# The first mixer's transposed probabilities: all copies out of PSUM by ScalarE

## The chip, the cores and the metric

The kernel runs on one core of one Trainium2 chip. The metric is device time in microseconds of one execution: three runs of the kernel before took 2435.21, 2437.50 and 2441.94 us, a median of 2437.5. A fourth execution was profiled; all rows below are from it. The engines are TensorE (PE, with its weight loads as PEld), VectorE (DVE), ScalarE (ACT), GpSimd (POOL) and SyncE (SP, which issues the weights' DMAs).

## The reference

Two blocks follow each other on 512 tokens of width 1024. The first is a gated convolution with an mLSTM and a feed-forward network. The second block has two layers, each with a mixer, an attention over 256 memory rows, an output projection and a feed-forward network. The first layer's mixer is sparse attention with three branches, twelve heads of 64 in four groups:

```python
p_s = _masked_softmax(s_s, mask_s[:, :, None])
o_s = jnp.einsum('bgrqk,bgqkd->bqgrd', p_s.astype(vg.dtype), vg)
...
p_w = _masked_softmax(s_w, mask_w)
o_w = jnp.einsum('bgrqk,bkgd->bqgrd', p_w.astype(vwc.dtype), vwc)
...
return gc[:, :, 0] * o_c + gc[:, :, 1] * o_s + gc[:, :, 2] * o_w
```

The second layer's mixer is a recurrence over the tokens (RWKV-7, twelve heads): `state = state * w_t + sa * b_t + v_t * k_t`, read out with `r_t`. Everything is float32.

## The kernel before

Activations lie transposed in SBUF, 128 channels to a tile of 128x512. A float32 product with a weight is three products of split operands (high by high, high by low, low by high); these are the dense products, with `wh` and `wl` in their names. Weights come through SyncE's queue; ScalarE makes `wh`, VectorE `wl`.

Each mixer has a projection of dense products, side work (the mixer itself) and the output projection `_wo` (L1765) in three parts: the first needs the results 0 and 1 of the mixer and the memory attention, the second needs 2 and 3, the third 4 and 5. Side work is written as generators in a list (`_Side`, L407). After every few dense products the planner lets the generator run whose inputs are due first; where `_wo` lacks a result, it only steps side work.

What is due when is told by the planner's own clock (`_Clock`, L246), which adds a modelled duration for every instruction on its engine as it is written (ScalarE and VectorE have different ones) and notes who wrote and read what. That clock runs through the whole program. Its times decide the order in which instructions are written, and every engine then executes its own instructions in that order.

The clock also decides on idle products. Inside a mixer, `keep_warm` (L533) issues a 128x512 product of a tile of zeros into a bank that nobody reads, either until the time at which the next side work is due, or until a count that the planner keeps is reached:

```python
while self.zps is not None and (self.pe + 300 < until or not (until or self.clock.hot(HOTF))):
    self.nc.tensor.matmul(self.zps, self.zero[:, 0:128], self.zero, start=True, stop=True)
```

The first mixer (`_nsa`, L1699) makes six items of two heads. Each has, for two branches and four blocks of 128 queries, a unit `_nsa_unit` (L1614), 48 in all: products with the keys, a minimum and an exponential, a division by the sum with the gate, transposes of the probabilities into PSUM, copies to SBUF, products with the values. A unit of query block b covers n = 128(b+1) keys. For b of 0 and 1 both heads' probabilities share one bank; for b of 2 and 3 there are two banks and two copies. The line `if (i2 + b) % 2` (L1650) gives the copies in turn to VectorE (`vcopy`) and ScalarE (`acopy`).

The second mixer (`_rwkv`, L2178) makes six pairs of heads (`_rw_pair`, L1973). The steps of a pair that the prediction speaks of, in order: preparation; products for a 64x64 block matrix; the block inverse `_rw_inv` (L1933), which goes to DRAM (`ltd`), comes back, takes 30 small VectorE steps and a ScalarE copy, and goes through DRAM (`img`) once more; transposes of v; two levels of products that complete the inverse; products that apply it; products with `eye`; a recurrence of seven steps, each a product and a VectorE multiplication with `fs`; the read-out, its statistics (VectorE, GpSimd's power, ScalarE), transposes, a gate product, and a split into high and low parts (`hl_g`, L594) that `_wo` takes.

All instructions of the mixers are recorded through one helper, so all have the line L365 in the profile; they are told apart by tiles and shapes. In names, s is an SBUF tile, b a PSUM bank, wh and wl the split weights, fs the recurrence's factors, st, mv and gt the statistics. The idle product is `b<-s` with one s.

Of the kernel before, what the change touches and what calls it, by code (L numbers as in the profile page):

```python
# [1613 lines left out]
def _nsa_unit(B, i, br, b, st, P, mix):  # L1614

    nc = B.nc
    t = i // 3
    n = 128 * (b + 1)
    ks, vs = ("ks", t) if br == 0 else ("kw", t), ("vs", t) if br == 0 else ("vw", t)
    while not ("po" in P and ks in st and vs in st):  # L1620
        yield
    k, v = st[ks], st[vs]
    sm = B.mp.tile([128, 4], F32, tag="sm", name="sm", bufs=8)
    one = n <= 256
    held = [B.sl.get() for _ in range(1 if one else 2)]
    pr = [held[0][:, 0:n], held[0][:, n:2 * n] if one else held[1][:, 0:n]]
    for hf in range(2):
        ps = B.ps.get()
        q = P["q"][hf][:, 128 * b:128 * b + 128]
        B.mm(ps[:, :n], q, k[hf][:, 0:n], True, False)  # L1630
        B.mm(ps[:, :n], q, k[2 + hf][:, 0:n], False, True)
        nc.vector.tensor_tensor_reduce(pr[hf], ps[:, :n], P["strip"][hf][:, S - n:], 1.0, 3.0e38,
                                       op0=OP.add, op1=OP.min, accum_out=sm[:, 2 + hf:3 + hf])
        B.act(pr[hf], pr[hf], AF.Exp, bias=sm[:, 2 + hf:3 + hf], scale=-1.0, accum=sm[:, hf:hf + 1])
        B.ps.put(ps)
    yield
    g = 12 * (br + 1) + 2 * i
    nc.vector.reciprocal(sm[:, 0:2], sm[:, 0:2])
    B.tt(sm[:, 0:2], sm[:, 0:2], st["gts"][:, b, g:g + 2], OP.mult)
    for hf in range(2):  # L1640
        B.ts(pr[hf], pr[hf], sm[:, hf:hf + 1])
    yield
    ph = [B.sl.get() for _ in held]
    pt = [ph[0][:, 0:n], ph[0][:, n:2 * n] if one else ph[1][:, 0:n]]
    for i2 in range(len(held)):
        ps = B.ps.get()
        w = 2 * n if one else n
        for o in range(0, w, 128):
            B.tr(ps[:, o:o + 128], held[i2][:, o:o + 128], B.ident)
        if (i2 + b) % 2:  # L1650
            B.vcopy(ph[i2][:, :w], ps[:, :w])
        else:
            B.acopy(ph[i2][:, :w], ps[:, :w])
        B.ps.put(ps)
    B.sl.put(*held)
    yield
    P["n"][b] -= 1
    po = P["po"]
    for kb in range(b + 1):
        for hf in range(2):  # L1660
            B.mm(po[64 * hf:64 * hf + 64, 128 * b:128 * b + 128], v[:, kb, 64 * hf:64 * hf + 64],
                 pt[hf][:, 128 * kb:128 * kb + 128], False, sum(P["n"]) == 0 and kb == b)
    B.sl.put(*ph)
    if sum(P["n"]) == 0:
        B.sl.put(*P["q"], *P["strip"])
        yield
        mix[i] = yield from B.hl_g(po)
        B.ps.put(po)
# [30 lines left out]
def _nsa(B, xg, factors):  # L1699
# [9 lines left out]
    def project(n, ps):  # L1709
        t = B.sl.get()  # L1710
        if n == 18:
            B.tt(t[0:36], ps[0:36], rb[0:36], OP.mult)
            B.ps.put(ps)
            B.ts(t[0:36], t[0:36], B.col("gate_b", 0, 0, 36), None, OP.add)
            B.side.add(_nsa_gates(B, t, st))
        elif n in (19, 20) or n < 6:
            B.stt(t, ps, -0.125, rb, OP.mult, OP.mult)
            B.ps.put(ps)
            if n >= 19:
                B.side.add(_mem_att(B, 0, n - 19, t, cross), 6)  # L1720
            else:
                P = {"n": [2] * 4}
                B.side.add(_nsa_comp(B, n, t, st, P), 6)
                for br in range(2):
                    for b in range(3, -1, -1):
                        B.side.add(_nsa_unit(B, n, br, b, st, P, mix), 4 if b > 1 else 2)
        else:
            B.tt(t, ps, rb, OP.mult)
            B.ps.put(ps)
            nm, e = {6: "kc", 8: "vc", 10: "ks", 12: "vs", 14: "kw", 16: "vw"}[n - n % 2], n % 2  # L1730
            if nm in ("vs", "vw"):
                B.side.add(_tok_major(B, t, st, (nm, e)))
            elif nm in ("ks", "kw"):
                B.side.add(_stack_k(B, t, st, (nm, e)), 4)
            else:
                st[nm, e] = t
                if n == 9:
                    B.side.add(_compress(B, st), 4)
# [552 lines left out]
```

## Time and profile before

| what | value |
|---|---|
| median of three runs | 2437.5 us |
| profiled execution, its time | 2441.78 us |
| its span, first to last instruction | 2440.0 us |
| first mixer's units and projection in the span | about 1040 to 1262 us |
| second mixer, from its last projection to the third part | about 1770 to 2052 us |
| TensorE busy / granted clock, mean | 96% / 0.987 |
| VectorE, ScalarE, GpSimd busy | 59%, 38%, 13% |

A matmul's end is modelled and the next one begins before it, so a row's duration of about 0.4 us for a 128x512 product is not its share of TensorE's time; the distance between starts is. A float32 product that is not split stands as two instructions in the trace; a transpose stands as one.

### The profile page before, as it was taken

To read this page: it belongs to the slowest core of one execution; us is meant where nothing else is said; L and a number is where in the kernel's file an instruction comes from. 1 tells how busy PE (TensorE), PEld (TensorE's weight loads), DVE (VectorE), ACT (ScalarE), POOL (GpSimd) and SP (SyncE) were. 2 spreads that over 40 slices of the span, in tenths; PEclk is the share of its full clock that TensorE was granted. 3 is DMA by queue.
4 is the path that set the end of the run, shared out by engine and by line. 5 is a ranking of instruction groups with operands and counts; after the bars stand their busy time and mean duration, and the time that the engine had idled before them with its cause. 6 is when DMAs were issued, how large, how long until landed. Compare 5 with 4: busy or idle time off the path is not lost. (4 is left out here: it accounts for less than half of the span.)

```text
span 2440.0 us, 35941 instructions
## 1 busy us (share of the span) xinstructions
PE 2351.7 (96%) x14466; PEld 1919.4 (79%) x14466; DVE 1449.4 (59%) x2785; ACT 921.7 (38%) x1546; POOL 310.4 (13%) x291
## 2 busy tenths in 40 slices
PE   6999999899999999999999999999989899999997
PEld 5878887677888888877778888888868687888886
DVE  7977875776433335578885434446785666543443
ACT  5365455244222233346453222234343324322322
POOL 4333334200000002201001000021111200000000
PEclk9999999999999999999999999999998999999998
DMA  8222222744433323412213233244332141333322
GB/s 276 90 77 68 78 78 84 267 149 147 130 87 112 95 84 112 169 55 76 64 35 126 86 107 102 85 141 144 124 84 58 44 109 44 95 88 112 95 83 81
DMA packets 124711, 252.52 MB, mean 103 GB/s; under 512 B 48060, under 2 KB 54636, under 8 KB 124544
## 3 DMA queue, kind: packets, MB, share of 16 engines
q1 hardware_dynamic: 76096, 211.64, 27.9%
q0 software_dynamic: 10288, 32.48, 4.0%
q10 hardware_dynamic: 38160, 6.10, 1.4%
q8 instruction: 113, 1.85, 0.3%
q14 instruction: 54, 0.44, 0.1%
HBM read 234.43 MB, written 15.75 MB: 103 GB/s over the span
## 5 line engine op out<-in xcount | busy, mean ns | idle before, releaser
L365 PE MATMUL b<-s,wh 128*128 128x512 f32 (+1 forms) x5456 | 1687.5, 391 | 18.2 <-DVE s L365 11.4
L365 PEld LDWEIGHTS b<-s,wh 128*128 128x128 f32 x5456 | 1015.1, 189 | 234.4 <-DVE s L365 14.1
L365 PE MATMUL b<-s,wl 128*128 128x512 f32 (+1 forms) x2728 | 1060.1, 389 | 13.2 <-DVE wl L365 11.5
L365 PEld LDWEIGHTS b<-s,wl 128*128 128x128 f32 x2728 | 514.3, 189 | 122.0 <-DVE wl L365 15.1
L365 DVE TENSOR_TENSOR wl<-wr,wh 128x1024 fp32r<-128x1024 f32 (+2 forms) x313 | 356.2, 1140 | 221.1 <-ACT wh L365 219.8
L365 ACT ACTIVATE wh<-wr 128x1024 fp32r<-128x1024 f32 (+2 forms) x371 | 363.9, 983 | 231.2 <-PE b L365 176.9
L365 ACT ACTIVATE s<-s 128x512 f32<-128x512 f32 (+7 forms) x321 | 191.5, 611 | 626.1 <-DVE s L365 605.3
L365 DVE TENSOR_TENSOR s<-b,s 128x512 f32<-128x512 f32 (+3 forms) x314 | 196.9, 635 | 350.9 <-PE b L365 328.5
L365 DVE TENSOR_TENSOR s<-s,s 128x512 f32<-128x512 f32 (+12 forms) x466 | 239.3, 517 | 142.7 <-ACT s L365 132.7
L365 PE MATMUL b<-s,s 64*64 64x64 f32 (+5 forms) x4112 | 299.0, 257 | 16.5 <-DVE s L365 8.8
L365 PEld LDWEIGHTS b<-s,s 64*64 64x64 f32 (+2 forms) x4112 | 234.3, 145 | 78.4 <-issue 28.9
L365 ACT ACTIVATE s<-b 128x512 f32<-128x512 f32 (+4 forms) x227 | 107.1, 498 | 260.9 <-PE b L365 201.0
L365 DVE SCALAR_TENSOR_TENSOR b<-s,par,b 128x510 f32<-128x510 f32 (+28 forms) x288 | 193.2, 734 | 18.5 <-ACT b L365 17.2
L365 POOL TENSOR_TENSOR wl<-wr,wh 128x1024 fp32r<-128x1024 f32 x58 | 141.0, 2434 | 227.0 <-ACT wh L365 218.5
L365 POOL TENSOR_TENSOR s<-s,s 128x512 f32<-128x512 f32 (+1 forms) x38 | 44.3, 1187 | 428.9 <-ACT s L365 425.8
L365 PE MATMUL b<-ident,s 128*128 128x128 f32 (+1 forms) x520 | 76.7, 280 | 12.5 <-DVE s L365 8.4
L365 PEld LDWEIGHTS b<-ident,s 128*128 128x128 f32 (+1 forms) x520 | 59.5, 138 | 31.1 <-DVE s L365 13.1
L365 POOL TENSOR_TENSOR rs_t<-rs_t,mhalf 128x4 f32<-128x4 f32 (+1 forms) x8 | 10.7, 1334 | 560.7 <-DVE rs_t L365 560.7
L365 PE MATMUL b<-s 128*128 128x512 f32 x232 | 69.0, 426 | 0.0
L365 DVE SCALAR_TENSOR_TENSOR s<-s,par,s 128x512 fp32r<-128x512 f32 (+2 forms) x67 | 49.1, 747 | 30.5 <-ACT s L365 30.2
L365 ACT ACTIVATE s<-s,sm 128x512 f32<-128x512 f32 (+3 forms) x96 | 52.8, 552 | 36.8 <-DVE sm L365 36.3
L365 ACT ACTIVATE s<-b,par 128x512 f32<-128x512 f32 x54 | 37.3, 701 | 55.6 <-PE b L365 49.5
(161 smaller groups left out, 1138.5 us busy)
## 6 DMA issues: line engine op xcount, KB each, us to landing
wr<-in_w_in_dram SPq DMA_DIRECT2D x59, 512.0 KB, 3.5
s<-in_w_ada_dram SPq DMA_DIRECT2D x96, 256.0 KB, 5.4
wr<-in_fu_dram SPq DMA_DIRECT2D x44, 512.0 KB, 3.5
wr<-in_f0u_dram SPq DMA_DIRECT2D x44, 512.0 KB, 3.5
wr<-in_f1u_dram SPq DMA_DIRECT2D x44, 512.0 KB, 3.5
wr<-in_w_rw_dram SPq DMA_DIRECT2D x23, 512.0 KB, 3.9
wr<-in_w_nsa_dram SPq DMA_DIRECT2D x21, 512.0 KB, 3.6
wr<-in_w_o_dram SPq DMA_DIRECT2D x16, 512.0 KB, 3.6
```

The costliest lines, as they stand in the source:

```text
L365: r = f(*a, **k)
```

## The change

The choice of the engine is taken out; every copy is ScalarE's.

```diff
-        if (i2 + b) % 2:
-            B.vcopy(ph[i2][:, :w], ps[:, :w])
-        else:
-            B.acopy(ph[i2][:, :w], ps[:, :w])
+        B.acopy(ph[i2][:, :w], ps[:, :w])
```

36 copies move: all 24 that VectorE had of 128x512 and all 12 of 128x384. The planner's clock has other times from the first of them on, so what follows is written in another order, in both mixers. Without the idle products each engine but these two has as many instructions as before. Idle products: 232 before, 320 after. By place: first mixer 52 and 66; second mixer up to the first part's last products 131 and 166; in its last wait 49 and 88.

ScalarE's order, first units of the first mixer. The tiles s are the copies of transposed probabilities, b the banks they are in; `s,sm` rows are exponentials.

```order
 L365 ACTIVATE s_8047,sm<-s_8047,sm 128x128 x2
+L365 ACTIVATE s_8082<-b_8084 128x512
 L365 ACTIVATE s_8083<-b_8090 128x512
+L365 ACTIVATE s_8100<-b_8102 128x512
 L365 ACTIVATE s_8101<-b_8108 128x512
 L365 ACTIVATE s_8121<-b_8123 128x384
+L365 ACTIVATE s_8122<-b_8128 128x384
```

Both copies of a unit now stand one behind the other on ScalarE, and as many rows are gone from VectorE's order.

TensorE's order ahead of the first dense product of the second mixer's output projection, before. `b_12918<-s_12917` is the idle product, `k_11663` belongs to a pair's gate product, the 64x64 products to recurrences.

```order
L365 MATMUL b_16409<-k_11663,s_16192 128x512 x4
L365 MATMUL b_16418<-s_15232,s_15246 64x64
L365 MATMUL b_16418<-s_15232,s_14264 64x64
L365 MATMUL b_16457<-s_15728,s_15742 64x64
L365 MATMUL b_16457<-s_15728,s_14980 64x64
L365 MATMUL b_12918<-s_12917 128x512 x2
L365 MATMUL b_16463<-s_15231,s_15245 64x64
```

The same place after; the idle product is `b_12932<-s_12931`, the last row is the projection's first dense product.

```order
L365 MATMUL b_12932<-s_12931 128x512 x8
L365 MATMUL b_16254<-s_15500,s_16095 64x64 x16
L365 MATMUL b_16272<-k_11677,s_16088 128x512 x4
L365 MATMUL b_16281<-s_15269,s_15283 64x64
L365 MATMUL b_16281<-s_15269,s_14275 64x64
L365 MATMUL b_12932<-s_12931 128x512 x37
L365 MATMUL b_16324<-s_15992,s_15500 64x128 x8
L365 MATMUL b_16334<-s_15993,s_15500 64x128 x8
L365 MATMUL b_16367<-s_15850,wh 128x512
```

Runs of 8 and 37 idle products stand where there were 2.

TensorE's order at the end of the projection's second part, before: its last three dense products, and the fifth recurrence step of the last pair behind them.

```order
L365 MATMUL b_17702<-s_17198,wh 128x512
L365 MATMUL b_17702<-s_17199,wh 128x512
L365 MATMUL b_17702<-s_17198,wl 128x512
L365 MATMUL b_17710<-s_17210,s_17224 64x64
L365 MATMUL b_17710<-s_17210,s_16598 64x64
L365 MATMUL b_12918<-s_12917 128x512
```

The same place after: the second part's last dense products, and behind them the last pair's transposes of v.

```order
L365 MATMUL b_17410<-s_17231,wh 128x512
L365 MATMUL b_17410<-s_17230,wl 128x512
L365 MATMUL b_17427<-ident,s_15609 64x128 x4
L365 MATMUL b_17433<-ident,s_15609 64x128 x4
L365 MATMUL b_17441<-eye,s_15614 64x64 x2
```

Further on in the same wait, after: the last pair's second level, the fourth pair's gate product, and the products that apply the inverse, with idle products among them.

```order
L365 MATMUL b_12932<-s_12931 128x512 x6
L365 MATMUL b_17551<-s_17143,s_16839 64x64 x16
L365 MATMUL b_17569<-k_11677,s_17416 128x512 x4
L365 MATMUL b_17578<-s_17144,s_17485 64x64 x16
L365 MATMUL b_12932<-s_12931 128x512 x3
L365 MATMUL b_17600<-s_17439,s_17144 64x128 x8
L365 MATMUL b_17610<-s_17440,s_17144 64x128 x8
L365 MATMUL b_12932<-s_12931 128x512 x3
L365 MATMUL b_17623<-eye,s_15615 64x64
```

What stood ahead of the second part's last dense products, from the last pair's transposes to its fourth recurrence step, now stands behind them, and the last pair's block inverse comes 321 TensorE instructions (as the trace counts them, idle products left out) later than before.

## Rows read from the trace of the kernel before

**Rows 1.** The page's first part, busy time of each engine over the span.

```profile
PE 2351.7 (96%) x14466; PEld 1919.4 (79%) x14466; DVE 1449.4 (59%) x2785; ACT 921.7 (38%) x1546; POOL 310.4 (13%) x291
```

**Rows 2.** Busy time by stretches of the first mixer: stretch, its length, then PE, PEld, DVE, ACT, POOL busy with the number of instructions, granted clock, DMA share, GB/s.

```profile
1050.00:1100.00 50.00, 49.23 (x324) 38.06 (x323) 40.65 (x133) 26.61 (x71) 0.00 (x0) 1.00 0.12 37
1100.00:1150.00 50.00, 47.90 (x339) 36.07 (x338) 42.88 (x135) 33.05 (x96) 6.52 (x12) 1.00 0.25 82
1150.00:1200.00 50.00, 49.19 (x340) 37.38 (x339) 43.85 (x127) 27.61 (x69) 2.69 (x5) 1.00 0.21 64
1200.00:1250.00 50.00, 47.60 (x318) 36.70 (x317) 42.74 (x141) 25.09 (x70) 1.60 (x3) 1.00 0.11 35
```

**Rows 3.** Groups of instructions by form in the first mixer, 1040 to 1270 us: busy us, mean ns of one, idle time before them. The two copies of VectorE, the like of ScalarE, the idle products.

```profile
L365 DVE COPY s<-b 128x512 f32<-128x512 f32 x24 | 16.4, 683 | 0.8 <-PE b L365 0.8
...
L365 PE MATMUL b<-s 128*128 128x512 f32 x52 | 15.0, 407 | 0.0
...
L365 ACT ACTIVATE s<-b 128x512 f32<-128x512 f32 x22 | 12.6, 594 | 5.1 <-PE b L365 5.0
...
L365 DVE COPY s<-b 128x384 f32<-128x384 f32 x12 | 6.6, 550 | 1.5 <-PE b L365 1.5
...
L365 ACT ACTIVATE s<-b 128x384 f32<-128x384 f32 x12 | 5.9, 491 | 3.1 <-PE b L365 2.9
```

**Rows 4.** TensorE's waits in the same stretch: for whom, us in total, times, longest.

```profile
PE b L365 <- DVE s L365: 3.3, 5, 1.6
PE b L365 <- ACT s L365: 1.1, 3, 0.7
```

**Rows 5.** Idle products: the group over the whole run, and three stretches of the timeline (start, length, count), the first at full clock, the others behind the wait at 1826.

```profile
L365 PE MATMUL b<-s 128*128 128x512 f32 x232 | 69.0, 426 | 0.0
```

```profile
2040.21 6.19 PE L365 MATMUL b<-s 128*128 128x512 f32 x26
```

```profile
1827.61 2.91 PE L365 MATMUL b<-s 128*128 128x512 f32 x6
...
1830.85 0.79 PE L365 MATMUL b<-s 128*128 128x512 f32 x1
```

**Rows 6.** The second mixer: busy time and granted clock of four stretches (columns as in rows 2), and the two long waits of TensorE in the timeline, with the wait in brackets and who ended it.

```profile
1820.00:1830.00 10.00, 3.90 (x31) 2.86 (x22) 9.04 (x34) 2.76 (x7) 0.21 (x1) 0.80 0.01 2
1830.00:1840.00 10.00, 10.00 (x81) 7.22 (x80) 3.37 (x9) 2.54 (x7) 1.09 (x3) 0.51 0.31 80
...
1940.00:1950.00 10.00, 1.75 (x4) 1.46 (x5) 5.97 (x31) 2.96 (x9) 4.27 (x6) 0.61 0.13 27
1950.00:1960.00 10.00, 10.00 (x78) 7.44 (x78) 6.68 (x11) 2.48 (x4) 3.94 (x9) 0.88 0.97 286
```

```profile
1826.89 1.06 PE L365 MATMUL b<-ident,s 128*64 128x128 f32 x4 [6.10 <-DVE s L365]
```

```profile
1948.25 0.80 PE L365 MATMUL b<-s,wh 128*128 128x512 f32 x1 [10.63 <-DVE s L365]
```

**Rows 7.** VectorE's timeline ahead of that second wait's end: the small steps of an inverse, another pair's statistics, the wait for GpSimd, the low part.

```profile
1934.71 8.15 DVE L365 TENSOR_TENSOR s<-s,s 64x15 f32<-64x15 f32 x32
...
1943.55 1.15 DVE L365 BATCH_NORM_STATS2 st<-b 128x6 f32<-128x64 f32 x8
...
1947.43 0.17 DVE L365 SCALAR_TENSOR_TENSOR gt<-mv,gt 128x8 f32<-128x8 f32 x1 [1.85 <-POOL gt L365]
1947.51 0.68 DVE L365 TENSOR_TENSOR s<-s,s 128x512 fp32r<-128x512 f32 x1
```

**Rows 8.** Busy time and TensorE instructions of the stretch that begins with the last pair's inverse (columns as in rows 2).

```profile
1983.00:1998.00 15.00, 15.00 (x306) 12.18 (x306) 12.43 (x43) 3.60 (x8) 0.00 (x0) 1.00 0.33 82
```

**Rows 9.** The last pair's chain in the timelines of VectorE, ScalarE and TensorE: the inverse, its copy, out to DRAM, back, the first masked product; the fourth pair's transposes; the last pair's products after its second `eye` bank; the last step with `fs`, statistics, scaling; the third part's first dense product.

```profile
1983.17 7.54 DVE L365 TENSOR_TENSOR s<-s,s 128x512 f32<-128x512 f32 x31
...
2004.19 0.69 DVE L365 TENSOR_TENSOR s<-b,s 128x512 f32<-128x512 f32 x1 [0.79 <-PE b L365]
...
2036.84 0.29 DVE L365 TENSOR_TENSOR s<-b,fs 64x128 f32<-64x128 f32 x1 [0.54 <-PE b L365]
2040.32 1.15 DVE L365 BATCH_NORM_STATS2 st<-b 128x6 f32<-128x64 f32 x8 [3.19 <-PE b L365]
```

```profile
1990.75 0.88 ACT L365 ACTIVATE s<-s 64x256 f32<-64x256 f32 x2 [7.27 <-DVE s L365]
...
1991.59 0.58 ACTq L365 DMA_DIRECT2D img<-s  x1
...
1998.19 2.79 ACTq L365 DMA_DIRECT2D s<-img  x4
...
2044.48 2.47 ACT L365 ACTIVATE s<-b,gt 128x64 f32<-128x64 f32 x8 [10.54 <-DVE gt L365]
```

```profile
2022.17 0.28 PE L365 MATMUL b<-ident,s 128*128 128x128 f32 x1
...
2024.14 0.27 PE L365 MATMUL b<-eye,s 64*64 64x64 f32 x1
...
2052.02 0.61 PE L365 MATMUL b<-s,wh 128*128 128x512 f32 x2
```

## The prediction

> **What bounds the kernel now.** I read the busy line first [rows 1]: TensorE works 96% of the span, VectorE 59%, ScalarE 38%. Where TensorE is full, only what changes its own queue or leaves it waiting can change the time. So the second view is the stage that is edited, in stretches of 50 us [rows 2]: in the first mixer TensorE is busy for 47.6 to 49.2 of 50 us at a granted clock of 1.00, VectorE for 40.7 to 43.9, ScalarE for 25.1 to 33.1. VectorE is close to full and ScalarE is not. The third view, the list of waits, says what this costs: TensorE waited 3.3 us for VectorE and 1.1 us for ScalarE in the whole mixer [rows 4]. That is 4.4 us that a better share between the two could win there, and no more.
>
> The fourth view is the program's order, since the edit alone does not tell what moves. The idle products (keep_warm) are issued by the planner where its own clock sees TensorE wait, and that clock has other numbers once 36 copies change engine. In the order I count 232 idle products before and 320 after: 52 and 66 in the first mixer, 131 and 166 in the second mixer up to the second part of its output projection, 49 and 88 in the last wait there. All other TensorE work is the same in number. The second mixer is not edited at all and is planned anew all the same. So the fifth view is that stage: it holds the same kind of products, 232 of them in the whole run and never waited for [rows 5], it has waits in it, 6.10 us at 1826.89 and 10.63 us at 1948.25 [rows 6], and its end hangs on a chain and not on TensorE's load [rows 9].
>
> **The change part by part.** Removed from VectorE: 24 copies of 128x512 at 683 ns and 12 of 128x384 at 550 ns, 16.4 + 6.6 = 23.0 us [rows 3]. Added to ScalarE: the same at 594 and 491 ns, 14.3 + 5.9 = 20.1 us. Neither engine is the bound there, so both count only through waits. Half of VectorE's 3.3 us may go, with 23 us taken off the 170 that it works in those 200 us [rows 2]: -1.6. ScalarE now takes both copies of a long unit one behind the other, where the two engines worked side by side: 24 second copies, each late by up to 594 ns, are 14.2 us if every one of them were waited for; the next unit's products stand between a copy and its use, so I take 0.4. The 14 more idle products: 26 in a row take 6.19 us, so one costs (6.19 - 0.41) / 25 = 0.23 us at full clock, 0.41 being the mean duration of one [rows 3, 5]; 14 x 0.23 = 3.2 us in an engine that is full. Sum for the first mixer: 3.2 - 1.6 + 0.4 = +2.0. Bounds: -4.4 (all waits go, the idle products fall into gaps) and 3.2 + 14.2 = +17.4.
>
> On ScalarE and VectorE the Trainium skill speaks against this edit: "PSUM — Partial Sum Buffer", section "Specifications (TRN2)", says that the two can read PSUM in parallel at full rate, and its section on engine instructions that each queue is strictly first in, first out. By these the pair of copies would lose its overlap, which is the 14.2 us of the upper bound; the waits of 1.1 us for ScalarE [rows 4] speak for little of it.
>
> Second mixer, up to the second part of its projection: 35 more idle products, 35 x 0.23 = +8.1. But before the first product of the projection TensorE now has runs of 8 and 37 of them where there were 2, and in that place it stood still for 10.63 us [rows 6]. The rows of VectorE tell why: the 32 small steps of a pair's block inverse (8.15 us from 1934.71), the statistics of another pair, 1.85 us of waiting for GpSimd, and only then the low half that the projection waits for [rows 7]. The new order has the inverse earlier, and 45 x 0.23 = 10.4 us of idle products cover it. So the gap goes, and with it the slow clock behind it: the granted clock was 0.61 over 1.75 busy us and 0.88 over the next 10 [rows 6], 0.7 + 1.2 = 1.9 us lost. 8.1 - 10.6 - 1.9 = -4.4; I leave 1.4 us for what is late next and take -3. Bounds: +8.1 (the gap stays and all idle products are paid) and -10.5 (the 6.10 us gap goes too).
>
> The tail. The last of the six pairs falls behind. Before, the last products of the projection's second part stand among this pair's recurrence; now they stand ahead of its transposes, its two inverse levels and everything after. Its block inverse is reached 321 TensorE instructions later, counted in both orders; 306 took 15.0 us there [rows 8], so 15.7 us later. From that inverse to the third part's first product the chain lasted 2052.02 - 1983.17 = 68.9 us [rows 9]: inverse, copy, two DMA trips, levels, the recurrence, statistics, GpSimd, ScalarE, the last product. From the levels on, 48 dense products stood in it, 48 x 0.23 = 11.0 us, and the fourth pair's transposes with what followed them, 2022.17 to 2024.14, 2.0 us. In the new order these stand earlier, beside the inverse and its DMA trips, so the chain can shrink to 56. It doesn't shrink so far: 39 more idle products stand in it (9.0 us), and the fourth pair's statistics now queue behind the inverse on VectorE, with its transposes and then the last pair's behind them on TensorE (up to 4 us). Between 56 and 69 I take 63: 15.7 + 63 - 68.9 = +9.8. Bounds: +2.8 and +15.8.
>
> The sum is 2.0 - 3.0 + 9.8 = +8.8 us. Every duration is from the profiled execution: 2441.8 us, a span of 2440.0 and 1.8 around it, so it would become 2450.6. The median of the three runs is 4.3 us lower, and the prediction is made from that: 2437.5 + 8.8 = 2446. The order shows no DMA of SyncE moved past another; GpSimd's loads keep their sequence. That the edit does not do what it says is ruled out: VectorE keeps 1 of the 37 such copies, which belongs to another helper.
>
> **The rivals.** A: nothing comes of it. The work that is left for TensorE after the inverse is smaller by just the 321 instructions, so if the chain can run at 57 the tail costs 15.7 + 57 - 68.9 = +3.8; with -3 ahead of it and 0 in the first mixer, +0.8: 2438. For it: TensorE had no wait from 1983 to 1998 [rows 8], so work that is moved ahead is not lost. Against it: the inverse, its copy and its DMA trips alone are 21.0 us from 1983.17 to the first masked product at 2004.19 [rows 9].
>
> B: faster. The place is the gap before the projection and the mixer ahead: all 4.4 us of waits in the first mixer go, with its 14 idle products paid (3.2), the 10.6 us gap and the 1.9 us of slow clock go, the 35 idle products lie in gaps, and the last pair is not late: -4.4 + 3.2 - 10.6 - 1.9 = -13.7: 2424. It decides if the tail costs less than 6 us and the idle products are free. For it: VectorE is the fuller engine in the edited stage; the slow products, 0.42 us apart at 1827.61, follow a gap [rows 5]. The Trainium skill leans this way twice: "Perfetto Trace Analysis", section "Optimizing Scalar/DVE Operations", lets work go to ScalarE where VectorE is saturated, and "TensorE: Matmul & The Clock Gate", part 1, says that activity is what releases the throttle, by which more idle products buy clock. Against it: the clock was 1.00 in the edited stage [rows 2], and below it only in a few places of the later one.
>
> C: the idle products are paid in full, all 88 of them, 20.2 us, because TensorE had no gap where they now stand: 2458. For it: TensorE is 96% busy. Against it: 10.63 + 6.10 us of gaps lie in just this stage.
>
> **How the numbers follow.** What a measurement of this kernel can tell from no change is about 0.3%, 7.3 us: below 2430.2 is faster, above 2444.8 slower. The forecast has 0.46 (0.33 slower, 0.13 within), A 0.25 (0.22 within, 0.03 faster), B 0.13 (0.11 faster, 0.02 within), C 0.16 (slower). So slower 0.49, within 0.37, faster 0.14. The forecast's own range is 2438 to 2455. The whole range is 2429 to 2460: it takes in A, most of C and the near side of B, and leaves some 0.1 below and 0.05 above.
>
> **What would show it.** In the profile after: 24 and 12 more ScalarE copies out of PSUM and none such on VectorE in the first mixer, TensorE's waits there still 2 to 5 us; no wait near 10 us before the projection, with a run of 37 idle products in its place; the last pair's inverse on VectorE beginning after the second part's products have been issued or among the last of them; and the time between that part's last product and the third part's first growing by 15 us or more. Wrong would be: a gap before the projection as long as before (then C), the last part reached earlier than before (then B), or a first mixer that grows or shrinks by more than 5 us, which the waits don't allow.

## The result and the profile after

The changed kernel takes 2466.2 us (median of four runs, 2464.3 to 2467.9), the kernel before 2436.4 (four runs, 2430.9 to 2441.9): a ratio of 1.012, 95% interval 1.0106 to 1.0134, 29.8 us slower. The prediction said 2446 and a range up to 2460: the sign is right, the size is more than three times the forecast.

Where the time went can be followed at marks that both kernels have: the start of certain dense products in TensorE's timeline, found by counting in the order. A block is one tile of weights, 24 dense products; the output projection's first part has four of them, the second and the third have two each. Times in us from the span's start, in the profiled executions.

| mark | before | after | difference |
|---|---|---|---|
| first product of the first mixer's projection | 949.1 | 947.4 | -1.7 |
| first product of the first feed-forward network | 1271.5 | 1272.2 | +0.7 |
| last block of the second mixer's projection | 1769.1 | 1769.9 | +0.8 |
| output projection, first part, second block | 1962.6 | 1968.0 | +5.4 |
| output projection, second part, last block | 2021.5 | 2023.9 | +2.4 |
| output projection, third part | 2052.0 | 2075.7 | +23.7 |

The edited stage grows by 2.4 us and the unedited second mixer by 22.9 us; from there the difference stays within 1.2 us of that to the end. The two profiled spans differ by 22.5 us and the medians by 29.8, because the profiled execution of before was long in the second mixer (the last section).

The busy line of the changed kernel, which answers [rows 1]: TensorE's share is still 96%. Busy time alone tells nothing here, since idle products are counted in it.

```profile
PE 2374.4 (96%) x14554; PEld 1933.1 (79%) x14554; DVE 1430.6 (58%) x2749; ACT 938.9 (38%) x1582; POOL 310.1 (13%) x291
```

The edited stage of the changed kernel in stretches of 50 us (columns as in [rows 2]), then its waits of TensorE (as in [rows 4]) and three groups by form (as in [rows 3]):

```profile
1050.00:1100.00 50.00, 48.93 (x335) 37.92 (x335) 35.54 (x126) 31.81 (x86) 0.54 (x1) 1.00 0.10 33
1100.00:1150.00 50.00, 48.71 (x345) 37.57 (x345) 39.35 (x125) 35.21 (x101) 6.95 (x13) 1.00 0.26 83
1150.00:1200.00 50.00, 48.76 (x330) 37.63 (x327) 39.52 (x117) 29.38 (x72) 2.67 (x5) 1.00 0.18 63
1200.00:1250.00 50.00, 48.01 (x302) 35.26 (x300) 37.33 (x128) 28.22 (x78) 0.61 (x2) 1.00 0.11 35
```

```profile
PE b L365 <- ACT s L365: 2.0, 5, 0.6
PE b L365 <- DVE s L365: 1.8, 3, 0.9
PE b L365 <- DVE sm L365: 0.8, 1, 0.8
```

```profile
L365 PE MATMUL b<-s 128*128 128x512 f32 x66 | 18.4, 407 | 0.0
...
L365 ACT ACTIVATE s<-b 128x512 f32<-128x512 f32 x46 | 25.2, 593 | 1.4 <-PE b L365 1.2
...
L365 ACT ACTIVATE s<-b 128x384 f32<-128x384 f32 x24 | 10.4, 485 | 1.5 <-PE b L365 1.4
```

VectorE has lost its copies (170.1 busy us in these 200 became 151.7), ScalarE has 46 and 24 where it had 22 and 12, each as long as before. TensorE waits about as long as before (4.6 us against 4.4 in these rows), less for VectorE and more for ScalarE, and has 14 more idle products.

The second mixer ahead of the output projection, in TensorE's timeline of the changed kernel up to the projection's first product. Before, TensorE came to that product at 1936.41, and the 10.63 us wait of [rows 6] stood behind the projection's first four products; first before, then after:

```profile
1936.41 0.74 PE L365 MATMUL b<-s,wh 128*128 128x512 f32 x2
1936.99 0.40 PE L365 MATMUL b<-s,wl 128*128 128x512 f32 x1
1937.23 0.40 PE L365 MATMUL b<-s,wh 128*128 128x512 f32 x1
```

```profile
1907.56 0.66 PE L365 MATMUL b<-ident,s 128*128 128x128 f32 x4 [1.48 <-ACT s L365]
...
1910.85 0.33 PE L365 MATMUL b<-s,s 64*64 64x64 f32 x4 [1.55 <-ACT s L365]
...
1916.04 2.37 PE L365 MATMUL b<-s,s 64*64 64x64 f32 x32 [2.77 <-DMA s<-img]
...
1932.74 8.65 PE L365 MATMUL b<-s 128*128 128x512 f32 x37
1941.33 1.96 PE L365 MATMUL b<-s,s 64*64 64x128 f32 x32
1943.22 0.74 PE L365 MATMUL b<-s,wh 128*128 128x512 f32 x2
```

The long wait is gone, and 37 idle products take 8.65 us, ahead of the projection's first product and not behind it. Ahead of them are new waits, and TensorE is busy for 23.40 us of the 30 from 1900, at a granted clock of 0.83:

```profile
1900.00:1930.00 30.00, 23.40 (x465) 19.12 (x465) 13.27 (x42) 8.26 (x21) 7.65 (x13) 0.83 0.45 113
```

The last pair's chain in the changed kernel, to be read beside [rows 9]: VectorE's timeline, then ScalarE's, then TensorE's.

```profile
2009.32 6.94 DVE L365 TENSOR_TENSOR s<-s,s 64x15 f32<-64x15 f32 x30
...
2016.90 0.68 DVE L365 TENSOR_TENSOR s<-s,s 128x512 fp32r<-128x512 f32 x1
2017.50 1.15 DVE L365 BATCH_NORM_STATS2 st<-b 128x6 f32<-128x64 f32 x8
...
2021.25 0.17 DVE L365 SCALAR_TENSOR_TENSOR gt<-mv,gt 128x8 f32<-128x8 f32 x1 [1.86 <-POOL gt L365]
...
2035.19 0.69 DVE L365 TENSOR_TENSOR s<-b,s 128x512 f32<-128x512 f32 x1 [1.20 <-PE b L365]
...
2064.02 1.15 DVE L365 BATCH_NORM_STATS2 st<-b 128x6 f32<-128x64 f32 x8 [1.58 <-PE b L365]
```

```profile
2016.35 0.64 ACT L365 ACTIVATE s<-s 64x256 f32<-64x256 f32 x1 [6.72 <-DVE s L365]
2021.51 0.70 ACT L365 ACTIVATE s<-b,gt 128x64 f32<-128x64 f32 x2 [4.52 <-DVE gt L365]
2021.88 0.58 ACTq L365 DMA_DIRECT2D img<-s  x1
```

```profile
2017.63 0.50 PE L365 MATMUL b<-s,wh 128*128 128x512 f32 x1 [3.49 <-DVE s L365]
...
2075.69 0.62 PE L365 MATMUL b<-s,wh 128*128 128x512 f32 x2
```

The inverse begins at 2009.32, 26.1 us later than the group at 1983.17 of [rows 9]; from there to the third part it is 66.4 us where it was 68.9. (That group has another operation in front. Its 30 small steps begin at 1983.78, so on equal terms it is 25.5 us, and 66.4 where it was 68.2.)

```profile
1983.78 6.94 DVE L365 TENSOR_TENSOR s<-s,s 64x15 f32<-64x15 f32 x30
```

So the chain is nearly as long as before and starts late, when little other work is left beside it: the stretch from the last block of the second part to the third part is 51.8 us where it was 30.5. TensorE's row at 2017.63 shows the inverse also holding up the projection itself for 3.49 us, since the low half that it needs (VectorE's row at 2016.90) stands behind the 30 small steps.

### The profile page after: what moved, and what is told of

Same layout as the page of the kernel before. It is cut to its first block, busy times and chain, and to the rows that moved or that the text cites. A ratio compares the mean times of both kernels' runs of the same rounds, so it can differ in the third digit from the quotient of the medians.

```text
span 2462.5 us, 36157 instructions
## 1 busy us (share of the span) xinstructions
PE 2374.4 (96%) x14554; PEld 1933.1 (79%) x14554; DVE 1430.6 (58%) x2749; ACT 938.9 (38%) x1582; POOL 310.1 (13%) x291
## 5 line engine op out<-in xcount | busy, mean ns | idle before, releaser
L365 PE MATMUL b<-s,wl 128*128 128x512 f32 (+1 forms) x2728 | 1060.1, 389 | 12.8 <-DVE wl L365 11.2
L365 DVE TENSOR_TENSOR s<-b,s 128x512 f32<-128x512 f32 (+2 forms) x314 | 196.7, 636 | 367.2 <-PE b L365 345.2
L365 ACT ACTIVATE s<-b 128x256 f32<-128x256 f32 (+4 forms) x263 | 124.2, 508 | 238.8 <-PE b L365 191.6
L365 PE MATMUL b<-s 128*128 128x512 f32 x320 | 92.2, 418 | 0.0
L365 PE MATMUL b<-ident,s 128*128 128x128 f32 (+1 forms) x520 | 76.2, 279 | 15.9 <-DVE s L365 10.8
L365 PEld LDWEIGHTS b<-s 128*128 128x128 f32 x320 | 58.8, 192 | 14.0 <-issue 1.7
L365 DVE SCALAR_TENSOR_TENSOR s<-s,par,s 128x512 fp32r<-128x512 f32 (+2 forms) x67 | 49.1, 748 | 30.3 <-ACT s L365 30.0
```

The costliest lines, as they stand in the source:

```text
L365: r = f(*a, **k)
```

## The experiments

Three theories stood against each other. Order: the second mixer's new order costs the time, and the moved copies cost nothing. Engines: the copies on ScalarE, or the first mixer's 14 more idle products, cost it. Idle: the idle products are paid in full. Eight kernels were run, each beside the kernel before on the same chip (its median was 2434.7 in the first four, 2435.2 in the others).

**1. The edit, with the second mixer in the old order.** At the start of the second mixer the planner's clocks of the two kernels differ by the same 1535.3 ns on every engine that computes. `shift` adds it to all times that the clock holds, and its second argument brings the count of the planner's current stretch to that of before.

```diff
     B.ratio, B.lat = RRATIO, RLAT
+    B.clock.shift(1535.3, 3584.0)
```

> The edited first mixer as it stands (its engines and its order), but the planner's clock is moved on by 1535.3 ns where the second mixer begins, to what it reads there in the kernel before; by that the second mixer gets the order of before, instruction for instruction. Order theory (the new order of the unedited second mixer costs the time): the edit keeps only the 2.4 us by which the first mixer grew between the two traces, so 2438 to 2441 us, and TensorE reaches the third part of the projection about 30 us after the sixth block of the second part, as before. Engine theory (the copies on ScalarE cost, or 14 more idle products in the first mixer): near the changed kernel, 2460 to 2468.

Measured: 2435.2 us, ratio 1.0008 (0.9993 to 1.0022), 3 us below the expected 2438 to 2441; the third part comes 30.5 us after the projection's sixth block, which is the second part's last. The loss is gone although every copy runs on ScalarE and the first mixer has its new order. The engine theory falls.

**2. The kernel before, with the second mixer in the new order.**

```diff
     B.ratio, B.lat = RRATIO, RLAT
+    B.clock.shift(-1535.3, -3584.0)
```

> The kernel before with not one copy moved; only the planner's clock is set back by 1535.3 ns where the second mixer begins, to what it reads there in the changed kernel, so that the second mixer gets the changed kernel's order. Order theory: slower by the 23 to 27 us that lie in the second mixer, 2460 to 2464. Engine theory: no change, 2434 to 2440.

Measured: 2465.0 us, ratio 1.0121 (1.0105 to 1.0137), 30.3 us slower without a single copy moved. That is the whole loss. It is even somewhat more than the 23 to 27 us expected, which were read against a profiled execution that was itself long in this stage (the last section).

**3. The copies moved, the whole order as before.**

```diff
+        if (i2 + b) % 2:
+            B.acopy_as_v(ph[i2][:, :w], ps[:, :w])
+        else:
+            B.acopy(ph[i2][:, :w], ps[:, :w])
...
+    def acopy_as_v(self, out, in_):
+        self.tc.nc.scalar.activation(out, in_, AF.Copy, bias=0.0, scale=1.0)
+        self.clock.note("vector", "tensor_copy", (out, in_), {})
```

> All 36 copies run on ScalarE, but the planner is told that the second ones ran on VectorE, so that the order of the whole program and its 232 idle products are those of before. Order theory: within 3 us of before, 2434 to 2440; the sign says whether the moved copies by themselves help (VectorE waited for less) or hurt (the pair in series). Engine theory: near the changed kernel, 2455 or more.

Measured: 2429.7 us, ratio 0.9974 (0.9965 to 0.9984), 5.0 us faster: below the expected band. TensorE's waits in the first mixer of this kernel:

```profile
PE b L365 <- ACT s L365: 1.3, 3, 0.9
...
PE b L365 <- DVE s L365: 0.2, 1, 0.2
```

Beside [rows 4], the 3.3 us of waiting for VectorE are gone and ScalarE's 1.1 have become 1.3. So the edit does help in its own stage, and two ScalarE copies in series are almost never waited for. The traces show it in the stage itself, from the first product of its projection to that of the feed-forward network. It is 322.4 us in the kernel before and in runs 2 and 7 (old copies, old order), 317.7 in runs 3 and 8 (copies moved, old order) and 324.7 to 324.8 in the changed kernel and in runs 1, 4, 5 and 6 (copies moved, new order). So the moved copies are worth -4.8 us there, and the first mixer's new order costs 7.1 us; between the medians of runs 1 and 3 it is 5.4.

**4. Half of the second mixer's idle products left out.**

```diff
+            self.idle += 1
+            z = (self.zps, self.zero[:, 0:128], self.zero)
+            if self.thin and self.idle % 2:
+                self.clock.note("tensor", "matmul", z, {})
+            else:
+                self.nc.tensor.matmul(*z, start=True, stop=True)
```

> The changed kernel in its own order, but every second idle product of the second mixer is not issued (the planner still counts it): 127 of 254 are left, fewer than the 180 of before. Nothing reads an idle product, so no part of the result is left out. Idle theory (each idle product is paid in full at 0.23 us): 127 x 0.23 = 29 us less, 2437. Order theory (they stand in waits for the last pair's chain): 2460 to 2466, or a few us more if the granted clock falls in the waits.

Measured: 2457.7 us, ratio to the kernel before 1.0088 (1.0073 to 1.0103), 8.5 us less than the changed kernel. 8.5 / 127 = 0.067 us for each product left out, where one in a full engine would cost 0.23. Neither theory is met exactly. TensorE's waits from 1770 to 2080 us, and its busy time and granted clock there, say where the rest went; first the changed kernel, then this one:

```profile
PE b L365 <- DVE s L365: 13.9, 8, 5.6
PE b L365 <- ACT s L365: 7.7, 6, 2.2
```

```profile
1770.00:2080.00 310.00, 282.98 (x4553) 223.72 (x4554) 186.23 (x550) 98.56 (x229) 38.55 (x54) 0.96 0.25 62
```

```profile
PE b L365 <- DVE s L365: 22.7, 14, 5.6
PE b L365 <- ACT s L365: 12.8, 12, 3.4
```

```profile
1770.00:2080.00 310.00, 268.71 (x4462) 212.08 (x4461) 193.26 (x560) 102.70 (x235) 38.63 (x54) 0.93 0.26 65
```

Waits for VectorE and ScalarE grow by 8.8 and 5.1 us: about half of what was taken out comes back as plain waiting. The granted clock falls too, from 0.96 to 0.93; over the whole execution it is 0.984 to 0.985 in the four executions of this run and 0.987 to 0.988 in the four of the changed kernel. By these rows that costs 0.07 x 268.7 - 0.04 x 283.0 = 7.5 us, an estimate. Of 29.2 us taken out, 13.9 and 7.5 so come back, which leaves about the 8.5 that were won. So 0.067 us is a net price in this stage: most idle products stand in waits, and they also kept the clock up. At this price the 74 more of the second mixer are 5.0 us of the 30, an estimate.

**5. Only the last pair's priority raised.**

```diff
-                B.side.add(_rw_pair(B, p, [st.pop(i, None) for i in range(3)], R, mix), 0, 10 - p)
+                B.side.add(_rw_pair(B, p, [st.pop(i, None) for i in range(3)], R, mix), 0, 10 - p + 2 * (p == 5))
```

> The changed kernel with one number more: the sixth pair's priority in the second mixer is raised by 2, so that it goes ahead of the fifth where both are ready. Late-pair theory (of the 30 us, some 21 are the last pair's chain, which stands alone between the second and the third part of the projection, 51.8 us in the changed kernel against 30.5): that stretch falls below 30 us and the total to 2438 to 2455 us, although nothing is put back to the order of before. Rival (what was lost is a good order as a whole, and no single pair): 2460 or more.

Measured: 2441.4 us, ratio 1.0021 (1.0008 to 1.0035): one number recovers 24.9 of the 29.8 us, with 31 more idle products in the second mixer than the kernel before has (211 in place of 180). The inverse on VectorE, and TensorE's way to the third part, in this kernel:

```profile
1969.44 7.28 DVE L365 TENSOR_TENSOR s<-s,s 128x256 fp32r<-128x256 f32 x31
```

```profile
2042.13 6.31 PE L365 MATMUL b<-s 128*128 128x512 f32 x27
2048.28 2.04 PE L365 MATMUL b<-k,s 128*128 128x512 f32 x8
2050.16 1.75 PE L365 MATMUL b<-s 128*128 128x512 f32 x7
2051.75 0.62 PE L365 MATMUL b<-s,wh 128*128 128x512 f32 x2
```

The inverse begins some 40 us earlier than in the changed kernel (the group's 31 steps are one split and the 30 of the inverse), and the last stretch is 15.9 us in place of 51.8. What is left of it is one pair's statistics and gate, covered by 27 and 7 idle products. The first part's second block comes 196.8 us after the projection's last block, nearly as late as in the changed kernel (198.2; 184.7 in run 1), so what this run wins back it wins behind that mark.

**6. The last two pairs raised.** As in run 5, with `10 - p + 3 * (p > 3)`.

> The changed kernel with the priorities of the fifth and the sixth pair raised by 3, ahead of the third and fourth. Late-pair theory: the second part's dense products, which the first four pairs feed, now stand behind the last two pairs' work and fill what was the tail; the stretch between the second part's last product and the third part's first falls near 10 us, and the total below the kernel before, 2415 to 2435. Rival (no single pair; or the wait only moves ahead of the projection): 2445 or more.

Measured: 2431.5 us, ratio 0.9983 (0.9971 to 0.9995). The third part now follows the last block of the second after 5.4 us, its own length: nothing is waited for at the end any more. The projection starts later (198.8 us after the mark at the projection's last block, where the changed kernel needs 173.4), and the mixer ends earlier all the same.

**7. The kernel before at a third phase of the clock.**

```diff
     B.ratio, B.lat = RRATIO, RLAT
+    B.clock.shift(600.0, 0.0)
```

> The kernel before, not one copy moved; the planner's clock is moved on by 600 ns where the second mixer begins, a value that neither kernel has. Phase theory (where the planner's clock stands against its own fixed 3413 ns windows at that point decides the order, and the kernel before stands at a good place): slower, with another order and another loss, 2445 to 2465, and the last pair late again. Rival (the changed kernel's phase is a single bad one): 2432 to 2440.

Measured: 2467.4 us, ratio 1.0124 (1.0102 to 1.0147), a little above the expected band. A shift by a value that neither kernel has costs 32 us. So the changed kernel's phase is not a single bad one. The last stretch is 41.1 us here, and the second part ends 20 us late too.

**8. The good halves together:** run 3's copies, run 6's priorities, the clock of the changed kernel in the second mixer.

```diff
+            B.acopy_as_v(ph[i2][:, :w], ps[:, :w])
...
+    B.clock.shift(-1535.3, -3584.0)
...
+                B.side.add(_rw_pair(B, p, [st.pop(i, None) for i in range(3)], R, mix), 0, 10 - p + 3 * (p > 3))
```

> What the runs so far say is good, together: the 36 copies on ScalarE with the first mixer in the order of before (2429.7), and in the second mixer the clock and the priorities of the run with the last two pairs raised. Late-pair theory: that run's time less some 5 us, 2410 to 2430, below both kernels. If the two gains are one and the same (both only free VectorE): no better than the run with the last two pairs raised.

Measured: 2421.5 us, ratio 0.9936 (0.9917 to 0.9955), 13.7 us below the kernel before and 44.8 below the changed one. Its busy line shows TensorE at 97% of a span of 2419.7 us:

```profile
PE 2347.4 (97%) x14504; PEld 1924.2 (80%) x14504; DVE 1428.6 (59%) x2749; ACT 936.4 (39%) x1582; POOL 309.6 (13%) x291
```

The gain over run 6 is 10 us, twice the expected 5. Between the two traces it is 13.1 us: 7.0 in the first mixer, since run 6 has the changed kernel's order there (the expectation counted only the copies' 5), and 5.4 in the second mixer, whose order is the same in both; why that stage was shorter was not tried.

The second mixer of all ten kernels, from the projection's last block (which is 0), in us:

| kernel | first part | second part, last block | third part | last stretch | idle products in the last stretch | median |
|---|---|---|---|---|---|---|
| before | 167.4 | 252.4 | 283.0 | 30.5 | 49 | 2436 |
| after | 173.4 | 254.1 | 305.8 | 51.8 | 88 | 2466 |
| run 1 | 158.7 | 245.0 | 275.5 | 30.5 | 49 | 2435 |
| run 2 | 172.8 | 253.5 | 305.3 | 51.7 | 88 | 2465 |
| run 3 | 160.5 | 247.2 | 277.7 | 30.5 | 49 | 2430 |
| run 4 | 167.2 | 248.8 | 297.3 | 48.5 | 44 | 2458 |
| run 5 | 171.4 | 265.9 | 281.8 | 15.9 | 34 | 2441 |
| run 6 | 198.8 | 269.0 | 274.5 | 5.4 | 0 | 2432 |
| run 7 | 173.0 | 272.2 | 313.3 | 41.1 | 73 | 2467 |
| run 8 | 197.9 | 263.7 | 269.1 | 5.4 | 0 | 2421 |

Runs 5 and 6 plan the whole stage anew with their priorities, so they don't show that the last pair's lateness alone, with all else unchanged, is worth 25 us. They show that orders in which the last pair is early have no long last stretch and are fast, even with more idle products and a later projection.

## Why the prediction was right in sign and wrong in size

Most of the signs that the prediction named came out: the copies, TensorE's waits in the first mixer, the 37 idle products, the growth of the last stretch. They test the mechanism and not the sizes. Two steps failed, the front of the second mixer by its mechanism and the tail by its size. Against the profiled execution of before they missed by 7.6 and 8.5 us. Most of the rest lies in that profile itself: its second mixer was 5.2 and 7.5 us longer than the same order took in runs 3 and 1.

**First mixer, +2.0.** The traces give +2.4, but that is luck: two terms were both too small and cancel. The VectorE waits were priced at -1.6, and 4.4 was called all that could be won; run 3 shows 4.8 us in the stage (5.0 between the medians; by its interval, 1.6 to 3.5 per mille, 3.9 to 8.5 us). TensorE's waits for the two engines fell by only 2.9 of that, from 4.4 to 1.5; where the rest comes from is open. The 24 second copies in series were taken as +0.4 with an upper bound of 14.2 (13.0, since 12 of them are of 128x384 and take 491 ns); run 3 shows next to nothing (1.3 us of waits for ScalarE in place of 1.1). The rule that the prediction quoted from the Trainium skill ("PSUM — Partial Sum Buffer", section "Specifications (TRN2)") on the two engines reading PSUM side by side does not decide here: the overlap that it describes was given up, and run 3 is faster. Against that stands the new order of the first mixer, 7.1 us, where the prediction counted 3.2 for the 14 idle products and nothing for waits that the order brings: TensorE waits for 4.6 us in the changed kernel and for 1.5 in run 3.

**Front of the second mixer, -3.** This is the step that failed first: "So the gap goes, and with it the slow clock behind it." The gap went, and the 37 idle products are where they were said to be. But a gap that is filled by idle products is not time won, and they do not even stand in that gap's place: it stood behind the projection's first four products, they stand ahead of the first. That first product came 6.0 us later than in the profiled execution before (14.7 and 12.8 later than in runs 1 and 3). From there to the first part's second block the changed kernel takes 24.8 us where it was 26.2, because other side work filled what had been the gap. What mattered was when the next result arrived, and TensorE's useful work was late: the first part's second block came 4.6 us later than in the profiled execution before, not 3 earlier. Against runs 1 and 3, which have the old order at a higher granted clock there, it is 13.5 and 10.9 us. The new waits at 1907 to 1916 and the stretch at clock 0.83 stand in this part; no run took them out alone, and run 4 takes 5.2 us of the loss back by leaving out 83 idle products up to there. No view of before could show these waits. The honest bound for an unedited stage that is planned anew was far above +8.1.

**The tail, +9.8.** The mechanism was right: the last pair late, and the third part waiting for its chain. One sign was not met: the inverse was to begin among the last products of the second part or behind them, and it begins 3.7 us ahead of that part's first product, at 2013.06. The size was off in two terms. The term that was mis-sized most is "its block inverse is reached 321 TensorE instructions later", 15.7 us by the mean of [rows 8]. The inverse came 26.1 us later: 5.4 us of it was late already at the first part's second block, the other 20.7 make 0.064 us for an instruction, not 0.049. The price came from a stretch full of short 64x64 products (85% of its products; 68% and 72% in the two stretches below). The stretch just ahead of it in the same trace gives 0.061, and the changed kernel's way from the second block to the inverse 0.060, with TensorE busy throughout; first before, then after:

```profile
1962.60:1983.10 20.50, 20.39 (x335) 16.58 (x333) 12.86 (x38) 9.12 (x21) 2.78 (x3) 1.00 0.32 79
```

```profile
1968.00:2009.30 41.30, 41.30 (x685) 31.39 (x682) 27.14 (x67) 10.25 (x24) 4.48 (x7) 1.00 0.25 70
```

The second term is the chain, taken as 63 us between 56 and 69, which measured 66.4. In it, the queueing that was priced at up to 4 us is the 4.9 us between the end of the inverse's copy (2016.99) and its first DMA out (2021.88): ScalarE issues both, and another pair's scaling stands between, waiting for VectorE, which waits for GpSimd. (In [rows 9] the DMA follows the copies at once.) The pair whose transposes the prediction calls the fourth is the last but one; it counts from 0. From the first part's second block to the third part the loss is 18.3 us, above the term's bound of 15.8.

**The rivals.** C (all idle products paid in full) gave 2458 and was the nearest in size, for the wrong reason: run 4 shows 0.067 us net for one in the second mixer, at which 88 of them are 5.9 us and not 20.2 (an estimate). B was right on VectorE's waits, and in that idle products keep the clock up (run 4: 0.96, and 0.93 with half of them left out); its gain in the second mixer did not come. A's "the chain can run at 57" did not hold. What was missing was a rival of another kind: that the order before is a good one, so that a replanning of the second mixer can lose some tens of us by itself. Runs 2 and 7 show two such orders, at +30 and +32; how many orders are as good was not tried. For this a sign stood in the kernel itself: a clock with fixed steps that runs through the whole program, so that a shift by 1.5 us upstream reaches a stage that nobody edits.

## What to carry to other kernels

Where a planner's clock runs through the program, split an edit into what it does on the engines and what it does to the order, by telling the planner the old cost: here the first is worth -5 us and the second +35. A stage that is replanned without being edited deserves a wide range that leans to the slow side, and terms such as "this gap goes" should be priced by when the next needed result arrives and not by how TensorE fills the time. When the end of a stage hangs on the last of several equal chains, raise that chain's priority first: it was worth more here than all copies.

## What the runs showed of the hardware

The same order took different times. From the second mixer's last projection block to the first part, the kernel before took 167.4 us in its profile and run 3, instruction for instruction the same on TensorE, 160.5. The stretch in which most of it lies, first in the kernel before, then in run 3, 4.7 to 5 us earlier in its span:

```profile
1820.00:1850.00 30.00, 23.84 (x409) 19.24 (x402) 18.85 (x57) 10.87 (x30) 1.84 (x4) 0.77 0.18 42
```

```profile
1815.00:1845.00 30.00, 25.44 (x492) 20.44 (x492) 19.85 (x56) 12.29 (x35) 1.84 (x4) 0.89 0.21 47
```

The granted clock of this stretch, a mean of parts at the full level of 2.4 GHz and at the half level of 1.2 GHz, was 0.77 in one and 0.89 in the other. In both TensorE had just waited for 6.1 us ([rows 6]; 6.09 in run 3); why the slow part was longer in one is open. A profiled execution of before can thus be several us long in one stage by the clock alone, and a loss read against it comes out too small: 22.5 us between the two profiled spans, 29.8 between the medians.
